# Four vector transpositions pinned to their place in the program, and three matmuls of sums for norms asked for two weight chunks later, in a four-stage decoder trunk in float32

## The chip, the cores and the metric

One core of a Trainium2 chip runs the whole program. The metric is the device time in microseconds (us) of one execution; lower is better. Three runs of the kernel before took 2047.09, 2047.10 and 2047.97 us, so the median is 2047.1 us. The profile comes from one more execution of the same program, which took 2048.53 us.

## The reference, cut to what matters

256 positions of width 2048 pass through two layers. Each layer adds to the residual `x` a mixer and a gated feed-forward network (FFN) with a causal convolution of width 3; layer 1 is the second one. A norm needs, for each position, the sum of the squares of `x` over its 2048 columns.

```python
for l in range(DEPTH):                       # DEPTH = 2
    h = rmsnorm(x, g_mix[l])
    # l = 0: chunked spatial gating, l = 1: latent attention; both beside memory attention
    x = x + concatenate([main, mo]) @ w_out[l]
    x = x + conv_ffn(rmsnorm(x, g_ffn[l]), w_ffn_up[l], conv_w[l], conv_b[l], w_ffn_down[l])
return rmsnorm(x, g_final)

def conv_ffn(h, w_up, cw, cb, w_down):       # w_up 2048 x 11264, w_down 5632 x 2048
    a = h @ w_up
    c = sum(pad(a)[:, k:k + S] * cw[k] for k in range(3)) + cb
    gate, val = c[..., :5632], c[..., 5632:]
    return (silu(gate) * val) @ w_down
```

## The kernel before, in words

**Chunks of weights.** Every large product reads its float32 weights from HBM once, in chunks of 256 x 512 numbers (512 KB). The method `chunk` (lines 93 to 118) handles one: the sync engine (SP) issues the load into a buffer `raw` (line 101), the scalar engine (ACT) writes a rounded copy `whi` (line 110; lines 115 and 116 where a gain is multiplied in), and the vector engine (DVE) writes the rest `wlo` (line 111). There are four buffers of each of the three kinds. A `raw` buffer can be loaded again when `wlo` of the chunk in it is done; a `whi` or `wlo` buffer can be written again when TensorE (PE) has finished the chunk in it.

**Products.** `gemm_fm` (line 155) multiplies a chunk pair at a time: 32 matmuls with the two `whi` (lines 147 and 148, sixteen for the first chunk and then sixteen for the second), then 16 with the two `wlo` (line 150). A product over 2048 rows and 512 columns is eight chunks, that is four pairs. In this text its chunks are called chunk 0 to chunk 7. Its result lies in two PSUM banks and is taken away after the last pair by `evict`.

**Hooks.** `gemm_fm` takes `hooks`, a table from a chunk's number to functions. They are called after the pair that holds this chunk has been written into the program, so hook 1 stands behind the first pair, hook 3 behind the second. They are how small work (scores, sums, copies) is put between chunks.

**The FFN** (`ffn`, line 582) goes through 11 groups of 512 gate columns and 512 value columns, in parts of 4, 4 and 3 groups. A group is two products with `w_ffn_up`: first the gate columns, then the value columns. Evicting a product runs `scaled` (line 228, DVE: PSUM times the norm's factor `rbc`, into `a`), one activation for each 128 columns (line 600, ACT, `c`), two multiply-adds for each (line 603, DVE, `c`), and for the value columns the product with the gate (line 616) and its split (lines 237 and 238). After a part come its products with `w_ffn_down`.

**Sums for norms.** Behind each product with `w_out` in layer 1 and layer 0, and behind each `w_ffn_down` product of layer 0's last part, DVE adds the result to the residual (line 554), and GpSimd (POOL) squares it (line 268, `sq`) and adds it to `ssum` (line 273). `rstd_bc` (line 260) adds `ssum` over the partitions by one matmul with ones (line 262; two passes in the profile) and derives `rbc` from it (lines 252 to 257, five steps on DVE and a square root on ACT, line 253). `rbc` is first read when the first product that needs it is evicted.

**The residual in token order.** The output is needed with tokens on the partitions. While `ffn` runs for layer 1, `x` is therefore transposed: `turn(h)` (line 961) has two DVE transpositions of 32 x 32 blocks (line 965) which write half `h` into the tile `small`, of which there is one buffer; `place(h, q)` (line 967) then issues 8 small transfers of 32 KB from `small` to the tile `xt`, on SP's queue (line 972). The table `turns` (line 1034) hands them to the value products of groups 1 and 2 of layer 1's FFN: `turn` at hook 0, the four `place` at hooks 1, 3, 5 and 7. That makes 4 transpositions and 64 small transfers. `xt` is first read when the first `w_ffn_down` product of layer 1 is added to it (line 978).

**Order.** What an engine executes in which order is not the written order: a scheduler simulates the program and moves an instruction ahead of others on its engine when the data it reads are there. In this kernel the transpositions depend only on the finished residual. A region marked `manual_schedule` keeps its written order, and so does a single instruction handed to `keep_in_program_order`. Each engine then runs its list strictly in order, and an instruction that waits holds up everything behind it on its engine; SP's list holds both the loads of weights and the small transfers.

Of the kernel before, what the change touches and what calls it, by code (L numbers as in the profile page):

```python
# [17 lines left out]
D = 2048  # L18
# [9 lines left out]
KR = 512  # L28
# [43 lines left out]
class Kernel:  # L72
# [510 lines left out]
    def ffn(self, l, after=None, to_tokens=None, tokens=None):  # L583
        nc, t = self.nc, self.t
        rb = self.tmp(self.cp, [P, S], "rbc", 2)
        xhl, ssum = self.xhl, self.ssum
        first = {1: [lambda: self.rstd_bc(rb, ssum, D)]}
        up, down = t["w_ffn_up"][l], t["w_ffn_down"][l]
        with self.tc.tile_pool(name=self.uid("ff"), bufs=1) as fp:
            g0 = 0  # L590
            for part, ng in enumerate(FF_GROUPS):
                h = self.ap.tile([P, NB, 512], F32R, tag="big", name=self.uid("h"))

                def conv(b, acc):
                    a = self.tmp(fp, [P, 2, S], "a", 2)
                    self.scaled(a, acc, rb)
                    c = self.tmp(fp, [P, 2, S], "c", 3)
                    for i in range(2):
                        w = lambda j: self.cT[:, l, j, b + i : b + i + 1]
                        nc.scalar.activation(c[:, i, :], a[:, i, :], AF.Identity, scale=w(2), bias=w(3))  # L600
                        for j in (1, 0):
                            o = c[:, i, 2 - j :]
                            nc.vector.scalar_tensor_tensor(o, a[:, i, : S - 2 + j], w(j), o, ALU.mult, ALU.add)  # L603
                    return c

                for g in range(g0, g0 + ng):
                    gate = self.tmp(fp, [P, 4, S], "gate", 2)

                    def eg(b, acc):
                        c = conv(4 * g + b, acc)  # L610
                        nc.scalar.activation(gate[:, b : b + 2, :], c, AF.Silu)

                    def ev(b, acc):
                        c = conv(FB + 4 * g + b, acc)
                        hv = self.tmp(fp, [P, 2, S], "hv", 2)
                        nc.vector.tensor_tensor(hv, gate[:, b : b + 2, :], c, ALU.mult)
                        j = 4 * (g - g0) + b
                        self.split_pair(h[:, j : j + 2, :], hv)

                    ks = list(range(NB))  # L620
                    turns = to_tokens[g - 1] if to_tokens is not None and g in (1, 2) else {}
                    self.gemm_fm(self.rows(up, g * 512, 512), ks, 4, lambda k: xhl[:, k, :], eg, hooks=first if g == 0 else {})
                    self.gemm_fm(self.rows(up, FF + g * 512, 512), ks, 4, lambda k: xhl[:, k, :], ev, hooks=turns)
                last = part == len(FF_GROUPS) - 1
                if last and l == 0:
                    self.new_hl()
                dn = down[g0 * 512 : (g0 + ng) * 512]
                for j in range(4):
                    src = self.rows(dn, j * 512, 512)
                    if tokens is not None:  # L630
                        self.gemm_tm(
                            src, 4 * ng, 512, lambda k: h[:, k, :], lambda tb, acc: tokens(j, tb, acc, last), late=3 if last and j == 3 else 0
                        )
                        continue

                    def ed(b, acc):
                        self.add_residual(4 * j + b, acc)
                        if last:
                            after(4 * j + b)

                    self.gemm_fm(src, list(range(4 * ng)), 4, lambda k: h[:, k, :], ed)
                g0 += ng
# [92 lines left out]
    def layer_b(self):  # L735
        nc, t, tc = self.nc, self.t, self.tc
        xhl, ssum = self.xhl, self.ssum
        rb = self.tmp(self.cp, [P, S], "rbc", 2)
        w, wkv = t["w_in_b"][0], t["w_kv_a"]
        gm = lambda k: self.gain("g_mix", NB + k)  # L740
        gk = lambda k: self.gain("g_kv", k)
        ks = list(range(NB))
        x = lambda k: xhl[:, k, :]
        mm, tt = nc.tensor.matmul, nc.vector.tensor_tensor
        with tc.tile_pool(name="lb", bufs=1) as lb:
# [8 lines left out]
            def latent(name):  # L754
                lat = lt.tile([P, 4, S], F32, name=name)
                sums = lt.tile([P, S], F32, name=name + "s")

                def evict(b, acc):
                    self.scaled(lat[:, b : b + 2, :], acc, rb)
                    self.square_add(sums, lat[:, b : b + 2, :], b == 0, self.cp)  # L760

                def finish(dst, n, gain):
                    r = self.tmp(lt, [P, S], "lr", 2)
                    self.rstd_bc(r, sums, n)
                    for b in range(4):
                        tt(lat[:, b, :], lat[:, b, :], r, ALU.mult)
                        self.split_gain(dst[:, b, :], lat[:, b, :], self.gain(gain, b))

                return evict, finish
# [8 lines left out]
                return r  # L778

            ek, fk = latent("ck")  # L780
            self.gemm_fm(self.rows(wkv, 0, KR), ks, 4, x, ek, gain=gk, hooks={1: [lambda: self.rstd_bc(rb, ssum, D)]})
            eq, fq = latent("ql")
            self.gemm_fm(self.rows(w, 0, QR), ks, 4, x, eq, gain=gm, hooks={4: [lambda: fk(chl, KR, "g_kv_lat")]})

# [21 lines left out]
            hooks = {2: [rotary_key], 5: [lambda: fq(qhl, QR, "g_q_lat")]}  # L806
# [128 lines left out]
            hooks = {0: each(attend, 8, 9) + each(turn, 10, 11), 2: each(attend, 10, 11)}  # L935
# [3 lines left out]
    def run(self):  # L939
        nc, tc, t = self.nc, self.tc, self.t  # L940
# [8 lines left out]
        with tc.tile_pool(name="fin", bufs=1) as fin:  # L949
# [9 lines left out]
            small = {}  # L959

            def turn(h):
                small[h] = self.tmp(fin, [P, 8, 2, 4, 32], "small", 1)
                for j in (0, 4):
                    src = self.x[:, 8 * h + j : 8 * h + j + 4, :].rearrange("p j s -> p (j s)")
                    nc.vector.transpose(small[h][:, j : j + 4].rearrange("p j a b c -> p (j a b c)"), src)

            def place(h, q):
                lanes = lambda i: slice(32 * i, 32 * i + 32)
# [37 lines left out]
            def tokens(j, part, acc, last):  # L1006
# [26 lines left out]
            call = lambda f, *a: lambda: f(*a)  # L1033
            turns = [
                {0: [call(turn, 0)], 1: [call(place, 0, 0)], 3: [call(place, 0, 1)], 5: [call(place, 0, 2)], 7: [call(place, 0, 3)]},
                {0: [call(turn, 1)], 1: [call(place, 1, 0)], 3: [call(place, 1, 1)], 5: [call(place, 1, 2)], 7: [call(place, 1, 3)]},
            ]
            self.ffn(1, to_tokens=turns, tokens=tokens)
# [46 lines left out]
```

## Time and profile before

| What | Value |
|---|---|
| Median of three runs | 2047.1 us (2047.09 to 2047.97) |
| The profiled execution's own time | 2048.53 us |
| Span in the profile, first to last instruction | 2046.8 us |
| PE busy | 2036.8 us |
| DVE busy | 1356.2 us |
| ACT busy | 1044.0 us |
| POOL busy | 94.2 us |
| Mean rate of the transfers | 193 GB/s |
| Mean granted TensorE clock | 0.999 |

A row of the timeline reads: start in us from the span's beginning, length in us, engine, line of the kernel, operation, what it writes and reads, count of merged instructions, and in brackets the idle time before it and what ended that. "SPq" is SP's sequencer, which issues transfers; the length there is the time of issuing, and the landing comes later. A row of the waits reads: engine and line, what it waited for, total us, number of times, longest. A row on one source line reads: line, engine, operation, names, count, then the shortest, the median and the longest duration in ns.

### The profile page before, as it was taken

The numbers are of one execution on the slowest core, as the hardware profiler recorded it, in microseconds if no ns is written. First come the engines' busy times: TensorE is split into PE (matmuls) and PEld (weight loads), VectorE is DVE, ScalarE is ACT, GpSimd is POOL, SyncE is SP. The second block draws the span as 40 slices with busy tenths as digits, with TensorE's granted clock in tenths as the row PEclk, the third lists the DMA queues.
The fourth block names the chain that finished last, engine by engine and source line by source line (L and its number), as shares of the span: only waits on it lengthen the run. The fifth ranks groups of instructions, "written<-read, shape, count | busy, mean of one in ns | idle before, by whom it ended". The sixth has DMA issues, their size and how long they took to land.

```text
span 2046.8 us, 39055 instructions
## 1 busy us (share of the span) xinstructions
PE 2036.8 (100%) x16232; PEld 1970.7 (96%) x16232; DVE 1356.2 (66%) x1859; ACT 1044.0 (51%) x1345; POOL 94.2 (5%) x125
## 2 busy tenths in 40 slices
PE   9999999999999999999999999999999999999998
PEld 8989999999999999999999999999988999889997
DVE  6855667767556666457688875776655667656665
ACT  6754644555435554345555665455544455434553
POOL 0000013000000000000052001300000000000000
PEclk9999999999999999999999999999999999999999
DMA  8675565666656666566665545786666666666654
GB/s 309 192 225 176 155 197 187 197 196 188 204 187 194 196 194 197 188 196 195 187 196 181 174 129 176 198 224 196 195 195 193 190 198 193 194 195 188 196 185 155
DMA packets 220626, 394.62 MB, mean 193 GB/s; under 512 B 31648, under 2 KB 38176, under 8 KB 220320
## 3 DMA queue, kind: packets, MB, share of 16 engines
q1 hardware_dynamic: 220160, 391.60, 62.0%
q8 instruction: 127, 2.08, 0.4%
q10 hardware_dynamic: 288, 0.52, 0.1%
q14 instruction: 51, 0.42, 0.1%
HBM read 387.88 MB, written 2.10 MB: 191 GB/s over the span
## 4 chain that ended last, share of the span: by engine, by line
PE 99%; POOL 0%; DVE 0%; issue 0%; ACT 0%; POOLq 0%
PE ps L150 26%; PE ps L147 26%; PE ps L148 26%; PE ps L178 6%; PE ps L179 6%; PE ps L180 6%; PE ps L865 0%; PE ps L485 0%; PE ps L484 0%; PE ps L487 0%; PE ps L548 0%; PE ps L513 0%; PE ps L688 0%; PE ps L898 0%; PE ps L867 0%; PE ps L288 0%
## 5 line engine op out<-in xcount | busy, mean ns | idle before, releaser
L111 DVE TENSOR_TENSOR wlo<-raw,whi 128x1024 fp32r<-128x1024 f32 (+1 forms) x672 | 817.5, 1233 | 615.7 <-issue 419.0
L110 ACT ACTIVATE whi<-raw 128x1024 fp32r<-128x1024 f32 (+1 forms) x672 | 705.2, 1056 | 800.3 <-PE ps L148 571.7
L147 PE MATMUL ps<-xhl,whi 128*128 128x256 f32 x3264 | 752.1, 277 | 0.0
L148 PE MATMUL ps<-xhl,whi 128*128 128x256 f32 x3264 | 750.6, 276 | 0.0
L147 PEld LDWEIGHTS ps<-xhl,whi 128*128 128x128 f32 x3264 | 612.8, 188 | 0.3
L148 PEld LDWEIGHTS ps<-xhl,whi 128*128 128x128 f32 x3264 | 612.6, 188 | 0.3
L150 PE MATMUL ps<-xhl,wlo 128*128 128x256 f32 x3264 | 404.3, 276 | 0.0
L150 PEld LDWEIGHTS ps<-xhl,wlo 128*128 128x128 f32 x3264 | 385.6, 188 | 0.2
L147 PE MATMUL ps<-h,whi 128*128 128x256 f32 x704 | 161.6, 276 | 0.0
L148 PE MATMUL ps<-h,whi 128*128 128x256 f32 x704 | 161.5, 276 | 0.0
L603 DVE SCALAR_TENSOR_TENSOR c<-a,cT,c 128x255 f32<-128x255 f32 (+1 forms) x352 | 146.3, 479 | 0.0
L179 PE MATMUL ps<-wlo,h 128*128 128x512 f32 (+1 forms) x364 | 139.0, 382 | 0.0
L180 PE MATMUL ps<-whi,h 128*128 128x512 f32 (+1 forms) x364 | 138.7, 382 | 0.0
L178 PE MATMUL ps<-whi,h 128*128 128x512 f32 (+1 forms) x364 | 138.3, 382 | 0.0
L147 PEld LDWEIGHTS ps<-h,whi 128*128 128x128 f32 x704 | 132.0, 188 | 0.0
L148 PEld LDWEIGHTS ps<-h,whi 128*128 128x128 f32 x704 | 131.9, 188 | 0.0
L600 ACT ACTIVATE c<-a,cT 128x256 f32<-128x256 f32 x176 | 91.6, 591 | 73.9 <-DVE a L228 73.9
L147 PE MATMUL ps<-mainhl,whi 128*128 128x256 f32 x512 | 118.0, 277 | 0.0
L148 PE MATMUL ps<-mainhl,whi 128*128 128x256 f32 x512 | 117.9, 276 | 0.0
L147 PEld LDWEIGHTS ps<-mainhl,whi 128*128 128x128 f32 x512 | 96.1, 188 | 0.0
L148 PEld LDWEIGHTS ps<-mainhl,whi 128*128 128x128 f32 x512 | 96.1, 188 | 0.0
L150 PE MATMUL ps<-h,wlo 128*128 128x256 f32 x704 | 86.9, 276 | 0.0
(246 smaller groups left out, 1973.6 us busy)
## 6 DMA issues: line engine op xcount, KB each, us to landing
raw<-in_w_ffn_up SPq DMA_DIRECT2D x352, 512.0 KB, 4.2
raw<-in_w_ffn_down SPq DMA_DIRECT2D x176, 512.0 KB, 4.7
raw<-in_w_out SPq DMA_DIRECT2D x64, 512.0 KB, 4.8
raw<-in_w_in_a SPq DMA_DIRECT2D x56, 512.0 KB, 4.3
raw<-in_w_mem_kv SPq DMA_DIRECT2D x30, 512.0 KB, 5.2
raw<-in_w_in_b SPq DMA_DIRECT2D x16, 512.0 KB, 3.9
raw<-in_w_uq SPq DMA_DIRECT2D x12, 384.0 KB, 3.2
raw<-in_w_kv_a SPq DMA_DIRECT2D x8, 512.0 KB, 3.8
```

The lines of the kernel that those rows point to most:

```text
L110: nc.scalar.activation(hi[:, :n], raw[:, :n], AF.Copy)
L111: nc.vector.tensor_tensor(lo[:, :n], raw[:, :n], hi[:, :n].bitcast(F32), ALU.subtract)
L147: mm(acc, wh, x[:, :S], start=first, stop=False)
L148: mm(acc, wh, x[:, S:], start=False, stop=False)
L150: mm(acc, wl, x[:, :S], start=False, stop=last)
L178: mm(acc, xh, wh, start=first, stop=False)
L179: mm(acc, xh, wl, start=False, stop=False)
L180: mm(acc, xl, wh, start=False, stop=last)
L600: nc.scalar.activation(c[:, i, :], a[:, i, :], AF.Identity, scale=w(2), bias=w(3))
L603: nc.vector.scalar_tensor_tensor(o, a[:, i, : S - 2 + j], w(j), o, ALU.mult, ALU.add)
```

## The change

Two hooks move from 1 to 3: the sum for the norm ahead of each FFN (used in both layers) and the one ahead of the shared key and value side. The four transpositions are handed to `keep_in_program_order`.

```diff
-        first = {1: [lambda: self.rstd_bc(rb, ssum, D)]}
+        first = {3: [lambda: self.rstd_bc(rb, ssum, D)]}
...
-            self.gemm_fm(self.rows(wkv, 0, KR), ks, 4, x, ek, gain=gk, hooks={1: [lambda: self.rstd_bc(rb, ssum, D)]})
+            self.gemm_fm(self.rows(wkv, 0, KR), ks, 4, x, ek, gain=gk, hooks={3: [lambda: self.rstd_bc(rb, ssum, D)]})
...
-                    nc.vector.transpose(small[h][:, j : j + 4].rearrange("p j a b c -> p (j a b c)"), src)
+                    tc.keep_in_program_order(nc.vector.transpose(small[h][:, j : j + 4].rearrange("p j a b c -> p (j a b c)"), src))
```

The engines' lists show what this moves. In the old list the first half was transposed and placed during the last products with `w_out` of layer 1, and the second half around the border to the FFN: on SP the 64 small transfers stood in runs of one to six between the loads. Now they stand in the two value products. SP's list in the value product of group 1, with both lists in one (minus: before; plus: after; raw_16553 and raw_16559 are the loads of its chunks 4 and 5, raw_16621 and raw_16627 those of chunks 6 and 7, raw_16718 and raw_16724 those of chunks 0 and 1 of group 2's gate product):

```order
 L101 DMA raw_16553<-in_w_ffn_up 128x2x512
 L101 DMA raw_16559<-in_w_ffn_up 128x2x512
+L972 DMA xt<-small_16474 32x8x32 x24
 L101 DMA raw_16621<-in_w_ffn_up 128x2x512
 L101 DMA raw_16627<-in_w_ffn_up 128x2x512
+L972 DMA xt<-small_16474 32x8x32 x8
 L101 DMA raw_16718<-in_w_ffn_up 128x2x512
 L101 DMA raw_16724<-in_w_ffn_up 128x2x512
```

24 small transfers now stand in one run between the loads of chunks 5 and 6, and 8 more behind chunk 7. Group 2's value product has the same, with the loads of its own chunks. On DVE, the two transpositions of a half stand between `wlo` of chunk 1 and `wlo` of chunk 2 of the same value product.

ACT's list around the border from group 1's value product to group 2's gate product (whi_16628 is chunk 7 of the value product, whi_16719, whi_16725, whi_16779 and whi_16785 are chunks 0 to 3 of the gate product, whi_16839 its chunk 4; line 600 evicts the value product):

```order
 L110 ACTIVATE whi_16628<-raw_16627 128x1024
 L110 ACTIVATE whi_16719<-raw_16718 128x1024
+L600 ACTIVATE c_16691<-a_16689,cT 128x256 x2
+L600 ACTIVATE c_16704<-a_16702,cT 128x256 x2
 L110 ACTIVATE whi_16725<-raw_16724 128x1024
 L110 ACTIVATE whi_16779<-raw_16778 128x1024
 L110 ACTIVATE whi_16785<-raw_16784 128x1024
-L600 ACTIVATE c_16691<-a_16689,cT 128x256 x2
-L600 ACTIVATE c_16704<-a_16702,cT 128x256 x2
 L110 ACTIVATE whi_16839<-raw_16838 128x1024
```

The four evicting activations moved ahead of the copies of chunks 1, 2 and 3. At the border from group 2 to group 3 they moved too, but only ahead of chunk 3.

PE's list in the first gate product of layer 1's FFN, before (ps_15608 and ps_15609 are the product's banks, wlo_15683 and wlo_15689 chunks 2 and 3):

```order
L150 MATMUL ps_15608<-xhl_14517,wlo_15683 128x256
L262 MATMUL ps_15670<-ssum_14518,ones 128x256
L150 MATMUL ps_15608<-xhl_14517,wlo_15683 128x256 x3
L150 MATMUL ps_15609<-xhl_14517,wlo_15683 128x256 x4
L150 MATMUL ps_15608<-xhl_14517,wlo_15689 128x256 x4
L150 MATMUL ps_15609<-xhl_14517,wlo_15689 128x256 x4
```

The same place now, where wlo_15672 and wlo_15678 are chunks 2 and 3:

```order
L150 MATMUL ps_15608<-xhl_14517,wlo_15672 128x256 x4
L150 MATMUL ps_15609<-xhl_14517,wlo_15672 128x256 x4
L150 MATMUL ps_15608<-xhl_14517,wlo_15678 128x256 x4
L150 MATMUL ps_15609<-xhl_14517,wlo_15678 128x256 x4
L262 MATMUL ps_15730<-ssum_14518,ones 128x256
L147 MATMUL ps_15608<-xhl_14517,whi_15742 128x256
```

The matmul of the sums went from behind the first of the pair's sixteen `wlo` matmuls to behind the last, the border of the second and third pair. In the two other places, layer 0's FFN and the key and value side, it moved to the same border.

## Prediction

> **What bounds the kernel now.** I read the head of the profile page first, then the chain that ended last, then what TensorE (PE) waited for.
>
> ```profile
> span 2046.8 us, 39055 instructions
> PE 2036.8 (100%) x16232; PEld 1970.7 (96%) x16232; DVE 1356.2 (66%) x1859; ACT 1044.0 (51%) x1345; POOL 94.2 (5%) x125
> ...
> PE 99%; POOL 0%; DVE 0%; issue 0%; ACT 0%; POOLq 0%
> ```
>
> ```profile
> PE ps L288 <- DVE ones L279: 1.1, 1, 1.1
> PE ps L262 <- POOL ssum L273: 1.0, 1, 1.0
> ```
>
> The chain is PE from end to end. Of its 10.0 us without work, one wait of 1.0 us in the middle of the program can be taken away; it is the one the change aims at. Whatever else the change does counts only if it makes PE wait where it doesn't wait now.
>
> **The moved matmuls of sums.** The timeline of PE around line 262 in layer 1, then in layer 0, then GpSimd's adds in layer 1.
>
> ```profile
> 1327.39 0.28 PE L150 MATMUL ps<-xhl,wlo 128*128 128x256 f32 x1
> 1328.71 0.70 PE L262 MATMUL ps<-ssum,ones 128*128 128x256 f32 x2 [1.04 <-POOL ssum L273]
> ```
>
> ```profile
> 359.32 0.28 PE L150 MATMUL ps<-xhl,wlo 128*128 128x256 f32 x1
> 359.44 0.59 PE L262 MATMUL ps<-ssum,ones 128*128 128x256 f32 x2
> ```
>
> ```profile
> 1325.18 3.48 POOL L273 TENSOR_TENSOR ssum<-ssum,sq 128x256 f32<-128x256 f32 x4
> ```
>
> Undisturbed, line 262 starts 0.12 us behind the matmul ahead of it (359.44 - 359.32); in layer 1 it took 1.32 us (1328.71 - 1327.39). The wait costs 1.2 us. The sums are complete at 1325.18 + 3.48 = 1328.66. The new place is fifteen matmuls later. These start 0.113 us apart by the page (32 + 16 of them fill a pair in 5.44 us: 1407.13 - 1401.69 below), so without the wait PE comes there at 1327.39 + 16 x 0.113 = 1329.2, after the sums. **Gain 1.2 us.** Layer 0 shows no wait to remove, and the third place is not in the list of waits: zero. The factor derived from the sums, in DVE's timeline:
>
> ```profile
> 1336.24 0.42 DVE L257 SCALAR_TENSOR_TENSOR rbc<-rbq,rbr 128x256 f32<-128x256 f32 x1
> ```
>
> It was ready at 1336.66, 8.0 us after line 262 began. In the new list one more `wlo` of 1.2 us stands ahead of it: 9.2 us. From the new place PE has two pairs left, 10.9 us, until the product ends whose eviction reads the factor. That hides it in all three places, so I take zero; if 1.7 us of cover are not enough somewhere, the eviction and not PE is late, since the next product has banks of its own. Bounds: zero and 1 us.
>
> **The transpositions on DVE.**
>
> ```profile
> L965 DVE STREAM_TRANSPOSE small<-xT x4: 1231/1232/1245, 1257.5 to 1325.4; 128x1024 f32<-128x1024 f32 x4
> ```
>
> ```profile
> 1379.28 2.36 DVE L111 TENSOR_TENSOR wlo<-raw,whi 128x1024 fp32r<-128x1024 f32 x2 [1.45 <-issue]
> 1384.72 1.23 DVE L111 TENSOR_TENSOR wlo<-raw,whi 128x1024 fp32r<-128x1024 f32 x1 [3.08 <-PE ps L150]
> ```
>
> In group 1's value product chunks 0 and 1 are done at 1381.64, and DVE then idles 3.08 us. Two transpositions take 2.46 us and fit: zero, and 1384.1 is when the small transfers may start. What leaves the products with `w_out` was off PE's path there, apart from the 1.2 us already counted.
>
> **The small transfers on SP, which decide.** First their issue, then one stretch of five and one of six with the loads beside them.
>
> ```profile
> L972 SPq DMA_DIRECT2D xt<-small x64: 585/608/1659, 1280.5 to 1355.9; - x64
> ```
>
> ```profile
> 1344.16 3.20 SPq L972 DMA_DIRECT2D xt<-small  x5
> 1347.46 0.55 SPq L101 DMA_DIRECT2D raw<-in_w_ffn_up  x1
> ```
>
> ```profile
> 1291.36 4.53 SPq L972 DMA_DIRECT2D xt<-small  x6
> 1295.99 0.55 SPq L101 DMA_DIRECT2D raw<-in_w_out  x1
> ```
>
> Five in a row hold SP 3.30 us up to the next load, 0.66 each; six, one of them slow, 4.63 us, 0.77 each. Before, a load stood behind every one to six of them. Now 24 stand ahead of chunk 6. What its load has to spare before the change, in SP's, ACT's and PE's timelines (the second fence is the landing of this one load, the last the start of PE's work on chunk 6 and on the next product):
>
> ```profile
> 1385.98 0.37 SPq L101 DMA_DIRECT2D raw<-in_w_ffn_up  x1
> ```
>
> ```profile
> DMA to landing us min/median/max: 3.6/3.6/3.6
> ```
>
> ```profile
> 1392.83 1.07 ACT L110 ACTIVATE whi<-raw 128x1024 fp32r<-128x1024 f32 x1 [1.45 <-PE ps L148]
> ```
>
> ```profile
> 1401.69 0.28 PE L147 MATMUL ps<-xhl,whi 128*128 128x256 f32 x1
> ...
> 1407.13 0.28 PE L147 MATMUL ps<-xhl,whi 128*128 128x256 f32 x1
> ```
>
> Chunk 6 was issued at 1385.98, landed 3.6 us later, its `whi` waited for a buffer, and PE began on it at 1401.69, 15.7 us after the issue. Landing and ACT's copy need 3.6 + 1.2 = 4.8 us (1.07 and my estimate of 0.1 for two hand-overs). So the load may be 10.9 us late (15.7 - 4.8).
>
> Now, in the old clock: the small transfers start at 1384.1 and 24 x 0.65 = 15.6 us later, at 1399.7, chunk 6 is issued. I take 0.65, near the stretch of five, since no load is mixed into the run. That is 13.7 us late: `whi` is ready at 1404.5, and **PE waits 2.8 us**. Chunk 7 goes out 0.6 us later and is needed 1.8 us later: no wait of its own. Then 8 more small transfers, 5.2 us: the next product's chunk 0 is issued at 1399.7 + 1.2 + 5.2 = 1406.1 and ready at 1410.9, while PE, 2.8 us late, is done with the pair at 1407.13 + 2.8 = 1409.95. **Second wait 0.95 us.**
>
> [...]
>
> At group 1's end the list of ACT adds a third. What stands ahead of chunk 1's copy there:
>
> ```profile
> 1407.63 1.28 DVE L228 TENSOR_TENSOR a<-ps,rbc 128x512 f32<-128x512 f32 x2
> ```
>
> ```profile
> 1408.35 2.08 ACT L600 ACTIVATE c<-a,cT 128x256 f32<-128x256 f32 x4 [1.76 <-DVE a L228]
> ```
>
> Line 600 started 1.2 us after the product's end (1408.35 - 1407.13) and takes 2.08 us. From 1409.95 and behind chunk 0's copy (1410.9) that gives 1413.0, and chunk 1's copy is done at 1414.1. PE needs it 16 matmuls, 1.8 us, after 1410.95: **third wait 1.3 us**. At group 2's end line 600 stands only ahead of chunk 3, needed 7.3 us after the product's end: zero. Group 2's value product otherwise repeats group 1's:
>
> ```profile
> 1422.80 2.36 DVE L111 TENSOR_TENSOR wlo<-raw,whi 128x1024 fp32r<-128x1024 f32 x2 [2.53 <-issue]
> 1428.24 1.23 DVE L111 TENSOR_TENSOR wlo<-raw,whi 128x1024 fp32r<-128x1024 f32 x1 [3.08 <-issue]
> ```
>
> ```profile
> 1445.21 0.28 PE L147 MATMUL ps<-xhl,whi 128*128 128x256 f32 x1
> ```
>
> DVE has the same gap, and chunk 6 is needed at 1445.21, 20.0 us after chunk 1's `wlo` (1425.16), as in group 1 (1401.69 - 1381.64 = 20.05).
>
> The sum: group 1 2.8 + 0.95 + 1.3 = 5.05; group 2 2.8 + 0.95 = 3.75; loss 8.8, gain 1.2, **net 7.6 us slower**. The profiled execution would span 2046.8 + 7.6 = 2054.4 and take 2048.5 + 7.6 = 2056.1; it lies 1.4 us above the median of the runs, so the median becomes 2047.1 + 7.6 = **2054.7 us**.
>
> Bounds: the landing of loads in this stretch,
>
> ```profile
> DMA to landing us min/median/max: 3.6/4.3/6.2
> ```
>
> is 4.3 us at the median. With that and 0.70 us an issue (between the two stretches), the first wait is 2.8 + 0.7 + 1.2 = 4.7 and the second 0.95 + 0.4 = 1.35: group 1 7.35, group 2 6.05, net +12.2, 2059.3. From below, 0.64 an issue gives a first wait of 2.6, and if everything behind it catches up nothing follows: 5.2 - 1.2 = +4.0, 2051.1.
>
> **The rivals.**
>
> *Not slower: the loads still come in time.* Chunk 6 needs its issue by 1385.98 + 10.9 = 1396.9, so 24 issues in 12.8 us, 0.53 us each, decide. Then only the gain is left: 2047.1 - 1.2 = 2045.9 us. For it: SP carried the same 64 transfers before and PE never waited for a load, and issues of a plain load take 0.37 us when SP is not pressed. Against it: the shortest of the 64 took 0.585 us, and they were spread among loads. Chance 0.10. [...]
>
> *The clock falls.* A cold PE is in the trace only at the start:
>
> ```profile
> 1.12 4.63 PE L288 MATMUL ps<-ones 128*128 128x128 f32 x20 [1.12 <-DVE ones L279]
> ```
>
> ```profile
> 6.10 0.42 PE L147 MATMUL ps<-memhl,whi 128*128 128x256 f32 x1
> 6.31 0.41 PE L148 MATMUL ps<-memhl,whi 128*128 128x256 f32 x1
> ...
> 7.28 0.63 PE L150 MATMUL ps<-memhl,wlo 128*128 128x256 f32 x4
> ```
>
> PE began at 1.12; at 6.10 its matmuls of 256 columns still started 0.21 us apart, from 7.28 on four took 0.63 us, the usual pace of 0.11. So about 6 us of work ran at half pace, 3 us lost. If the first wait of each group lets PE go cold like that, two times 3 us come on top: +13.6, 2060.7 us. For it: 2.8 us is over twice the longest wait now, and 4.7 in the upper bound. Against it: the wait of 1.04 us was not followed by a slow stretch. Chance 0.07. [...]
>
> **How the numbers follow.** My forecast, PE waiting for loads behind the small transfers, has 0.80 and spreads from 2051.1 to 2059.3; 0.03 is left for what I don't see. The range is 2051.0 to 2059.5: it holds the forecast and leaves the rest out. A measurement of this kernel can tell about 0.2% (4.1 us), so "same" is 2043.0 to 2051.2: that is the first rival and a sliver of the forecast, 0.11. Slower is 0.87: 0.79 of the forecast, 0.07 of the clock and a little of the rest. Faster has only 0.02, since no case gains 4 us.
>
> **What would show it.** Right: in the list of waits PE waits for ACT's `whi` (line 110) in group 1 and 2 and no more for `ssum`; SP's timeline has 24 small transfers in 15 to 17 us; four or five waits of PE lie between 1400 and 1460, the longest 2.5 to 5 us, at chunk 6. Wrong: chunk 6's load is issued before 1397, or PE has no wait there; or pairs behind a wait take about 11 us (the clock); or the waits lie elsewhere, on `wlo` or on the transpositions.

## The result and the profile after

Six runs of the changed kernel took 2063.43 us at the median (2060.46 to 2064.15); six of the kernel before, on the same chip, took 2047.53 us (2047.09 to 2048.95). The ratio is 1.0074, with a 95% interval of 1.0061 to 1.0087: 15.9 us slower. The forecast was 2054.7 us in a range of 2051.0 to 2059.5: the sign is right, the size is not.

The profiled execution of the changed kernel took 2062.12 us. Its head, and the shares of the chain that ended last:

```profile
span 2060.4 us, 39049 instructions
...
PE 2041.0 (99%) x16232; PEld 1973.9 (96%) x16232; DVE 1358.9 (66%) x1859; ACT 1043.7 (51%) x1345; POOL 94.4 (5%) x125
...
PE 96%; SPq 2%; DMA 1%; ACT 0%; issue 0%; DVE 0%; POOLq 0%; POOL 0%; ACTq 0%
```

The span grew by 13.6 us (2060.4 - 2046.8). PE has as many matmuls as before and is busy 4.2 us longer (2041.0 - 2036.8); the rest is idle. SP's queue and the transfers, which were not on the chain, now are. What PE waits for:

```profile
PE ps L147 <- ACT whi L110: 10.0, 3, 4.6
PE ps L288 <- DVE ones L279: 1.1, 1, 1.1
PE ps L147 <- ACT whi L132: 0.3, 1, 0.3
```

The wait for `ssum` is gone. Three waits for the `whi` of ACT's line 110, 10.0 us in all, are new. The short one at line 132 is no part of the change: an execution of the kernel before (e9 below) has 0.2 us there. SP's timeline in group 1's value product and, in the second fence, in group 2's:

```profile
1378.91 1.63 SPq L101 DMA_DIRECT2D raw<-in_w_ffn_up  x2
1382.45 17.01 SPq L972 DMA_DIRECT2D xt<-small  x24
1399.56 1.06 SPq L101 DMA_DIRECT2D raw<-in_w_ffn_up  x2
1400.67 5.22 SPq L972 DMA_DIRECT2D xt<-small  x8
1405.98 2.10 SPq L101 DMA_DIRECT2D raw<-in_w_ffn_up  x4
```

```profile
1435.30 16.32 SPq L972 DMA_DIRECT2D xt<-small  x24
1451.74 1.03 SPq L101 DMA_DIRECT2D raw<-in_w_ffn_up  x2
```

24 small transfers hold SP for 17.1 us (1399.56 - 1382.45) and 16.4 us (1451.74 - 1435.30). Only then do the loads of chunks 6 and 7 go out. This is chunk 6's load in group 1 from its issue to its landing, then ACT's timeline, then PE's:

```profile
DMA to landing us min/median/max: 4.1/4.1/4.1
```

```profile
1403.73 1.06 ACT L110 ACTIVATE whi<-raw 128x1024 fp32r<-128x1024 f32 x1 [12.06 <-DMA raw<-in_w_ffn_up]
...
1413.54 2.08 ACT L600 ACTIVATE c<-a,cT 128x256 f32<-128x256 f32 x4 [2.38 <-DVE a L228]
1415.53 1.99 ACT L110 ACTIVATE whi<-raw 128x1024 fp32r<-128x1024 f32 x2
```

```profile
1399.27 0.96 PE L150 MATMUL ps<-xhl,wlo 128*128 128x256 f32 x7
1404.84 0.58 PE L147 MATMUL ps<-xhl,whi 128*128 128x256 f32 x1 [4.61 <-ACT whi L110]
1405.22 0.42 PE L148 MATMUL ps<-xhl,whi 128*128 128x256 f32 x1
1405.43 0.41 PE L147 MATMUL ps<-xhl,whi 128*128 128x256 f32 x1
...
1410.34 0.39 PE L148 MATMUL ps<-xhl,whi 128*128 128x256 f32 x1
1410.56 0.29 PE L147 MATMUL ps<-xhl,whi 128*128 128x256 f32 x1
1410.69 0.28 PE L148 MATMUL ps<-xhl,whi 128*128 128x256 f32 x1
...
1413.07 0.28 PE L147 MATMUL ps<-xhl,whi 128*128 128x256 f32 x1
...
1416.63 0.39 PE L147 MATMUL ps<-xhl,whi 128*128 128x256 f32 x1 [1.58 <-ACT whi L110]
...
1457.04 0.39 PE L147 MATMUL ps<-xhl,whi 128*128 128x256 f32 x1 [3.84 <-ACT whi L110]
1457.26 0.28 PE L148 MATMUL ps<-xhl,whi 128*128 128x256 f32 x1
```

Issued at 1399.56, landed 4.1 us later, copied from 1403.73 to 1404.79, read by PE at 1404.84: each step waits for the one ahead of it. And PE starts again slowly. From 1404.84 its matmuls start 0.21 us apart (1405.22 to 1405.43), and only from 1410.56 on 0.11 to 0.13. The table by stretches shows the same; its columns after the length are busy time and count of PE, PEld, DVE, ACT and POOL, the granted clock, the share of the DMA engines and GB/s.

```profile
1395.00:1400.00 5.00, 5.00 (x47) 5.00 (x45) 0.00 (x0) 0.00 (x0) 0.00 (x0) 1.00 0.25 39
1405.00:1410.00 5.00, 5.00 (x24) 5.00 (x25) 2.27 (x2) 1.06 (x1) 0.00 (x0) 0.50 0.75 186
1420.00:1430.00 10.00, 10.00 (x90) 10.00 (x90) 8.94 (x10) 5.49 (x7) 0.00 (x0) 1.00 0.87 267
1457.00:1458.30 1.30, 1.26 (x11) 1.26 (x12) 1.23 (x1) 0.73 (x1) 0.00 (x0) 1.00 0.50 61
1458.40:1461.70 3.30, 3.30 (x18) 3.30 (x17) 1.23 (x1) 0.23 (x1) 0.00 (x0) 0.50 0.71 173
```

Ahead of the first wait, from 1395 to 1400, DMA moved 39 GB/s at a busy share of 0.25, while issues took SP 17.01 of the 17.1 us: the small transfers don't fill the engines, they fill SP's queue. Behind the wait the granted clock is 0.50, and 24 matmuls pass where 47 passed before. In group 2 PE starts again at 1457.04 at full clock; the clock falls only 1.3 us later and stays at 0.50 for 3.4 us. PE counts as busy there, so the list of waits shows nothing of it.

An undisturbed pair takes 5.44 us. In the changed kernel the pairs around the waits start at 1394.62, 1404.84, 1413.07 and 1420.40 in group 1 and behind it, and at 1447.60, 1457.04 and 1464.22 in group 2 and behind it. What a pair takes beyond 5.44 us is the loss, and the starts give the whole account, in us:

| Place | Forecast | Measured |
|---|---|---|
| Ahead of group 1 (wait for `ssum` gone; the rest is an earlier start) | -1.2 | -1.63 |
| Group 1, wait at chunk 6 | 2.8 | 4.78 |
| Group 1, half clock behind it | 0 | 2.79 |
| Group 1's successor, chunk 0 | 0.95 | 0 |
| The same, chunk 1 (line 600 ahead on ACT) | 1.3 | 1.89 |
| Group 2, wait at chunk 6 | 2.8 | 4.0 |
| Group 2, half clock behind it | 0 | 1.74 |
| Group 2's successor, chunk 0 | 0.95 | 0 |
| Sum | 7.6 | 13.57 |

That leaves 2.3 us between the 13.6 of the profile and the 15.9 of the medians: this execution lies 1.3 us below its median (2063.43 - 2062.12), and the profiled one of before 1.0 us above (2048.53 - 2047.53).

### The profile page after: what moved, and what is told of

It reads as the page before. It is cut to its first block, busy times and chain, and to the rows that moved or that the text cites. A ratio compares the mean times of both kernels' runs of the same rounds, so it can differ in the third digit from the quotient of the medians.

```text
span 2060.4 us, 39049 instructions
## 1 busy us (share of the span) xinstructions
PE 2041.0 (99%) x16232; PEld 1973.9 (96%) x16232; DVE 1358.9 (66%) x1859; ACT 1043.7 (51%) x1345; POOL 94.4 (5%) x125
## 4 chain that ended last, share of the span: by engine, by line
PE 96%; SPq 2%; DMA 1%; ACT 0%; issue 0%; DVE 0%; POOLq 0%; POOL 0%; ACTq 0%
PE ps L147 26%; PE ps L148 25%; PE ps L150 25%; PE ps L178 5%; PE ps L179 5%; PE ps L180 5%; SPq L972 2%; DMA raw<-in_w_mem_kv 0%; PE ps L865 0%; DMA raw<-in_w_ffn_up 0%; PE ps L548 0%; PE ps L513 0%; PE ps L485 0%; PE ps L484 0%; PE ps L487 0%
```

## The experiments

The theory: 24 issues in a row on SP make the load of chunk 6 late, PE waits for `whi`, and a wait past some length costs a slow stretch on top. Rivals: the burst of small transfers disturbs the loads in the DMA engines, not in SP's queue; the transpositions on DVE or the moved sums cost something themselves; the changed order of ACT's list does; the slow stretch comes of something else than the wait.

**The moved sums alone** (e1): the kernel before with the three hooks at 3, the transpositions not pinned.

```diff
-        first = {1: [lambda: self.rstd_bc(rb, ssum, D)]}
+        first = {3: [lambda: self.rstd_bc(rb, ssum, D)]}
...
-            self.gemm_fm(self.rows(wkv, 0, KR), ks, 4, x, ek, gain=gk, hooks={1: [lambda: self.rstd_bc(rb, ssum, D)]})
+            self.gemm_fm(self.rows(wkv, 0, KR), ks, 4, x, ek, gain=gk, hooks={3: [lambda: self.rstd_bc(rb, ssum, D)]})
```

> The kernel before with the three later hooks alone, nothing pinned. If the loss comes from the small transfers in one run on SP's queue: PE's wait of 1.0 us for ssum goes and nothing comes in its place, 1.2 to 1.6 us faster than before, about 2046.0 us. If the later sums cost something (a late eviction, a wait for the factor): slower than before, a part of the 16 us, 2050 us or more.

2047.29 us (2046.99 to 2047.87, 11 runs) against 2047.56 us (27 runs); ratio 0.9998, 0.9989 to 1.0007. Its span is 2045.6 us and its list of waits has one row:

```profile
PE ps L288 <- DVE ones L279: 1.1, 1, 1.1
```

The hooks do no harm. Their gain, 0.3 us between the medians, misses the 1.2 to 1.6 us expected and can't be told from nothing; on the wait that they were to remove see e9.

**The pin alone** (e2): the kernel before with the other part of the change.

```diff
-                    nc.vector.transpose(small[h][:, j : j + 4].rearrange("p j a b c -> p (j a b c)"), src)
+                    tc.keep_in_program_order(nc.vector.transpose(small[h][:, j : j + 4].rearrange("p j a b c -> p (j a b c)"), src))
```

> The kernel before with the four transpositions pinned, the hooks as they were. If the small transfers in one run on SP make the loss: as slow as the changed kernel, 2062 to 2065 us, with two waits of PE of 4 to 5 us at chunk 6 of the value products of groups 1 and 2; the wait for ssum may go here too, since DVE is free earlier. If the hooks have a part in the loss: clearly below 2060 us.

2061.93 us (2060.2 to 2062.82, 4 runs); ratio 1.0072, 1.0057 to 1.0088, against the same 27 runs.

```profile
PE ps L147 <- ACT whi L110: 9.4, 3, 4.5
```

```profile
1455.16 0.39 PE L147 MATMUL ps<-xhl,whi 128*128 128x256 f32 x1 [3.35 <-ACT whi L110]
```

The same three waits: the pin makes the loss by itself, 14.4 us here against 15.9 for the whole change, with ranges that overlap. By the starts of the pairs the waits at chunk 6 cost 4.67 and 3.5 us, the slow stretches behind them 1.5 and 1.7, the wait behind line 600 1.9. The second fence is the wait at chunk 6 in group 2: 3.35 us without work were followed by the half clock too, from 1455.5 to 1458.9. The wait for `ssum` is not in this list, though its hook is at 1 as before; on this see e9.

**No small transfers** (e3): the changed kernel with its transpositions on DVE and without the 64 transfers; `xt` holds zeros, so the output lacks the residual.

```diff
+            nc.gpsimd.memset(xt.rearrange("p a d -> p (a d)"), 0.0)
...
-                        nc.sync.dma_start(out=out, in_=small[h][lanes(q), :, tb, b, :])
+                        pass
```

> The changed kernel without the 64 small transfers (xt is filled with zeros instead, so the residual is left out of the output); the transpositions stay pinned. If SP's queue makes the loss: no wait of PE for whi, 1.2 to 1.6 us faster than before, about 2046 us. If the transpositions on DVE at their new place or the changed order of ACT make it: still 2055 to 2063 us.

2047.51 us (2047.31 to 2047.63, 10 runs); ratio 1.0, 0.9991 to 1.0009; span 2045.6, no wait for `whi` at line 110. The pinned transpositions cost nothing on DVE. Without the transfers the whole loss is gone. ACT's list is back in its old order here too; see the end of e8.

**The same transfers, spread** (e4): the changed kernel, with all 64 transfers on SP and pinned there a few at a time, some of them into the next group's gate product.

```diff
+            RUNS = [0, 4, 4, 4, 4, 4, 4, 8]
...
+            def piece(h, n):
+                q, b, tb = n // 8, n // 2 % 4, n % 2
...
+                tc.keep_in_program_order(nc.sync.dma_start(out=out, in_=small[h][lanes(q), :, tb, b, :]))
+
+            def run_of(h, i):
+                for n in range(sum(RUNS[:i]), sum(RUNS[: i + 1])):
+                    piece(h, n)
+
+            turns = [{0: [call(turn, h)], **{2 * i + 1: [call(run_of, h, i)] for i in range(4)}} for h in range(2)]
+            later = [{2 * i - 7: [call(run_of, h, i)] for i in range(4, 8)} for h in range(2)]
```

> The changed kernel with the same 64 small transfers on the same queue and at the same time of the program, but pinned in runs of 4 to 8 with two loads between the runs, over the value product and the next gate product. If the length of the run decides: the longest run takes 5.2 us of the 10.9 us that a load may be late, PE doesn't wait, about 2046 us. If the small transfers disturb the loads in the transfer engines wherever they stand: waits of PE in both groups, 2050 us or more.

2047.26 us (2046.65 to 2047.41, 11 runs); ratio 0.9998, 0.9989 to 1.0007; span 2045.2. SP's timeline in group 1's value product (line 1040 issues the small transfers here):

```profile
1382.44 5.31 SPq L1040 DMA_DIRECT2D xt<-small  x8
1387.84 1.06 SPq L101 DMA_DIRECT2D raw<-in_w_ffn_up  x2
1388.95 2.55 SPq L1040 DMA_DIRECT2D xt<-small  x4
1391.60 1.06 SPq L101 DMA_DIRECT2D raw<-in_w_ffn_up  x2
1392.71 2.76 SPq L1040 DMA_DIRECT2D xt<-small  x4
```

Four transfers and two loads take SP 3.8 us (1392.71 - 1388.95), less than a pair's 5.44, so the loads keep ahead. At the same number of transfers on the same queue the loss is gone with the long run.

**The transfers on another queue** (e8): the changed kernel with all 64 small transfers issued by GpSimd, the 32 of a half in one run.

```diff
-                        nc.sync.dma_start(out=out, in_=small[h][lanes(q), :, tb, b, :])
+                        nc.gpsimd.dma_start(out=out, in_=small[h][lanes(q), :, tb, b, :])
```

> The changed kernel with all 64 small transfers issued from GpSimd's queue, which is idle there; transpositions, hooks and data are the same, and the 32 of a half stand in one run with the loads flowing beside them. If the loss comes from SP being held by the issue: no wait of PE for whi, 2046.5 to 2048 us. If the burst of small transfers slows the loads in the transfer engines: waits of PE for whi in groups 1 and 2, 2050 us or more.

2047.70 us (2047.33 to 2048.01, 10 runs) against 2047.89 us (21 runs); ratio 0.9999, 0.999 to 1.0009; span 2045.8. From GpSimd's timeline:

```profile
1382.87 8.84 POOL L972 DMA_DIRECT2D xt<-small  x15 [56.97 <-DVE small L965]
1392.34 4.62 POOL L972 DMA_DIRECT2D xt<-small  x8 [0.63 <-DMA xt<-small]
```

The transfers go out at 0.59 us each from 1382.87 on, as in the changed kernel (1382.45), beside the loads, and PE has no wait for `whi`. The rival of the DMA engines falls: SP, held by issues, makes the loads late.

Something else goes along with the loss in e3, e4 and e8. As their traces show, line 600 stands behind the copy of chunk 3 again in their ACT lists, as in the kernel before. So these three take away the long run and the wait of 1.9 us behind line 600 together, and don't tell them apart. The waits at chunk 6 don't depend on that order: their load had not left SP until 1399.56.

**A shorter run** (e6, e7): the code of e4 with other counts; 20 and then 16 small transfers ahead of chunk 6, 8 behind chunk 7 and the rest behind the next product's chunk 1.

```diff
-            RUNS = [0, 4, 4, 4, 4, 4, 4, 8]
+            RUNS = [0, 0, 20, 8, 4, 0, 0, 0]
...
+            RUNS = [0, 0, 16, 8, 8, 0, 0, 0]
```

> The changed kernel with 20 small transfers ahead of chunk 6, 8 behind chunk 7 and 4 behind the next product's chunk 1, otherwise the same. If each transfer holds SP 0.65 us: the first waits shrink by 2.6 us to about 2.2 and 1.4 us, no slow pace behind them, a wait of about 1 us for chunk 0 and about 1 us for chunk 1 behind group 1; 2051 to 2055 us. If the loads are late for another reason: waits and time as in the changed kernel.

2054.36 us (2053.34 to 2056.61, 6 runs) against the 21 runs; ratio 1.0033, 1.002 to 1.0045. The wait list's row, PE's first two matmuls of chunk 6 in group 1, and the stretch behind them:

```profile
PE ps L147 <- ACT whi L110: 5.2, 4, 1.7
```

```profile
1402.18 0.38 PE L147 MATMUL ps<-xhl,whi 128*128 128x256 f32 x1 [1.71 <-ACT whi L110]
1402.40 0.28 PE L148 MATMUL ps<-xhl,whi 128*128 128x256 f32 x1
```

```profile
1402.00:1407.00 5.00, 4.73 (x39) 4.54 (x40) 2.45 (x2) 1.19 (x2) 0.00 (x0) 1.00 0.59 127
```

Four transfers fewer are 2.6 us at 0.65 each. The pairs of chunk 6 start 1.87 us (group 1) and 1.89 us (group 2) late instead of 4.78 and 4.0, that is 2.9 and 2.1 less. PE goes on at full pace at once, at clock 1.00: the wait of 1.71 us left no slow stretch. And the waits at the next product's chunk 0, which the changed kernel didn't show, are there: the pairs before it take 1.5 and 1.4 us too long (6.92 and 6.81 instead of 5.44). The time is inside the 2051 to 2055 us expected. The wait of about 1 us expected at chunk 1 behind group 1 did not come: only two of line 600's four activations stand ahead of that copy here.

> The changed kernel with 16 small transfers ahead of chunk 6, 8 behind chunk 7 and 8 behind the next product's chunk 1. By the same 0.65 us the first waits fall to nothing or under 1 us and the loads behind are at the border too; 2047 to 2050 us. If the loads are late for another reason: 2055 us or more.

2052.39 us (2052.03 to 2053.28, 10 runs); ratio 1.0023, 1.0014 to 1.0032. This missed the 2047 to 2050 us expected. SP's timeline:

```profile
1382.96 10.55 SPq L1040 DMA_DIRECT2D xt<-small  x16
1393.61 1.06 SPq L101 DMA_DIRECT2D raw<-in_w_ffn_up  x2
1394.72 5.64 SPq L1040 DMA_DIRECT2D xt<-small  x8
1400.45 1.06 SPq L101 DMA_DIRECT2D raw<-in_w_ffn_up  x2
1401.57 5.18 SPq L1040 DMA_DIRECT2D xt<-small  x8
```

Chunk 6 goes out at 1393.61, and in group 1 PE has no wait for it. But 8 transfers and two loads then take 6.85 us (1401.57 - 1394.72), over the 5.44 us of a pair, so the lateness grows from pair to pair and comes out at chunk 2 of the next product (0.8 us by the starts of the pairs). Group 2 waits 1.35 us at chunk 6, 1.38 at chunk 0 and 1.1 at chunk 2. The slack of 10.9 us is spent once; what follows has to fit a pair's time.

**PE kept at work** (e5): the changed kernel, with 16 matmuls of 128 x 128 ones between the pair of chunks 4 and 5 and that of 6 and 7, in both groups.

```diff
+            def warm():
+                acc = self.psum()
+                for i in range(16):
+                    tc.keep_in_program_order(nc.tensor.matmul(acc[:, :P], self.ones, self.ones, start=True, stop=True))
...
-                {0: [call(turn, 0)], 1: [call(place, 0, 0)], 3: [call(place, 0, 1)], 5: [call(place, 0, 2)], 7: [call(place, 0, 3)]},
+                {0: [call(turn, 0)], 1: [call(place, 0, 0)], 3: [call(place, 0, 1)], 5: [call(place, 0, 2), warm], 7: [call(place, 0, 3)]},
```

> The changed kernel with sixteen matmuls of ones by ones, about 3.4 us of work, put on PE between the pair of chunks 5 and 6 in both groups, where PE idles 4.8 and 4.0 us. If the slow pace behind the waits (2.8 and 1.7 us lost) comes from the idle time itself: chunk 6 starts when it did, the pace stays at 0.113 us a matmul, waits of about 0.9 us for the next product's chunk 0 come in its place, and the kernel gets 2 to 4 us faster than the changed one, 2059 to 2061.5 us. If the slow pace has another cause (the late buffers, the engines beside it): no faster than the changed kernel, 2063 us or more.

2060.92 us (2060.02 to 2061.84, 4 runs) against the 21 runs; ratio 1.0063, 1.0048 to 1.0078. PE's timeline at chunk 6 of group 1, and the stretch behind:

```profile
1400.50 3.73 PE L1036 MATMUL ps<-ones 128*128 128x128 f32 x32
1405.09 0.39 PE L147 MATMUL ps<-xhl,whi 128*128 128x256 f32 x1 [0.86 <-ACT whi L110]
1405.31 0.28 PE L148 MATMUL ps<-xhl,whi 128*128 128x256 f32 x1
```

```profile
1405.00:1410.00 5.00, 4.91 (x41) 4.91 (x42) 2.45 (x2) 1.10 (x2) 0.00 (x0) 1.00 0.76 157
```

Chunk 6 begins as late as in the changed kernel (1405.09 against 1404.84), but PE has filled the wait with work, and goes on at clock 1.00 with 41 matmuls in 5 us instead of 24. So it is the idle time (4.61 us in the changed kernel, 0.86 here) that brings the half clock. Group 1 loses 5.8 us instead of 9.5 (4.78 + 2.79 + 1.89). Of the 3.6 us less, 1.7 are the slow stretch less a new wait of 1.1 at chunk 0; most of the rest is not the matmuls' doing, for ACT's list has chunk 1's copy ahead of line 600 here, and the wait behind line 600 is gone. Group 2 loses 6.9 instead of 5.7: the slow stretch is gone there too, but its run of 24 began 0.87 us ahead of the product's first pair and not 1.42, so that chunk 6 cost 4.8 instead of 4.0, and waits at chunks 0 and 1 of 1.0 us each came out. The median lies 2.5 us below the changed kernel's 2063.43; each was taken beside its own runs of the kernel before, and against those the loss is 13.0 instead of 15.9 us.

**Before, once more** (e9): one further execution of the kernel before, unchanged.

> The kernel before once more, for its profile alone. The first profile had PE wait 1.0 us for ssum in an execution that took 1.4 us more than the median of the runs; the later hooks alone gained 0.3 us at the median and not 1.2. If the wait for ssum changes from execution to execution: an execution near 2047.2 us has a wait of under 0.3 us there, one near 2048.5 us again about 1 us. If the wait is the same in all of them: about 1 us whatever the time.

It took 2047.29 us, with a span of 2045.6. PE at line 262 in layer 1, and GpSimd's adds:

```profile
1327.44 0.28 PE L150 MATMUL ps<-xhl,wlo 128*128 128x256 f32 x1
1327.56 0.59 PE L262 MATMUL ps<-ssum,ones 128*128 128x256 f32 x2
```

```profile
1323.17 3.50 POOL L273 TENSOR_TENSOR ssum<-ssum,sq 128x256 f32<-128x256 f32 x4
```

The same program, without the wait: GpSimd's adds began 2.0 us earlier (1323.17 against 1325.18) and were done at 1326.67, ahead of the 1327.56 at which PE came. So the wait of 1.04 us belongs to some executions of this kernel and not to others. Of the 27 executions of the kernel before beside e1, ten took longer than the slowest of e1's eleven (2047.87 us). The later hooks may thus remove the wait where it occurs; that is suggested and not shown.

No version was shown to beat the kernel before: e1, e4 and e8 lie 0.2 to 0.3 us below it, each with 1 inside its interval. Those of e1, e3 and e4 were expected near 2046 and miss it by the gain that did not come.

## Why the prediction was wrong in size and right in sign

- **Right: the mechanism of the first waits.** Loads behind the run on SP are late and PE waits for `whi`; shown by e2 (the pin alone does it), e3 and e4 (no run, no loss), e8 (the run on another queue, no loss) and e6 (a run of 20, less loss). "Not slower: the loads still come in time" would have needed 0.53 us an issue; the median was 0.609, and a run of 24 came to 0.71 and 0.68 each.
- **Mis-sized: the first wait, 2.8 us forecast, 4.78 and 4.0 measured.** The step "I take 0.65, near the stretch of five, since no load is mixed into the run" was 1.5 us short in group 1: the row of the 64 issues had a longest one of 1659 ns, the stretch of six contained a slow one, and a run of 24 has more room for one than a run of five. One issue of the changed kernel took 1.84 us in group 1 and one 1.28 us in group 2; the others held 0.66. Landing took 4.1 instead of 3.6 us, another 0.5: the 3.6 was that of one load, while the median of the stretch, 4.3, was nearer. So 2.8 + 1.5 + 0.5 = 4.8. The upper bound, 4.7, was the better forecast.
- **The step that failed: the half clock put at nothing in the sum.** The wait and the clock were treated as separate cases, with 0.07 for the clock. That a wait of 2.8 us leaves the clock alone was the author's estimate: the longest wait in the trace of the kernel before is 1.1 us, and no profiled execution has one of 2.8. The two cases are one: the same terms that make the wait longer carry it to where the clock falls, and the forecast's own upper bound of 4.7 us lies above the 3.35 us at which e2 shows it. The half clock cost 2.79 + 1.74 = 4.5 us in the profile. Without it the profile's sum would be 9.0 us, or some 11 with the two waits at chunk 0 that e5 has in its place: both inside the forecast's 4.0 to 12.2. e5 shows that the idle time causes it, e6 that 1.7 us of it does not bring it.
  The traces set the border between two waits: 4.61, 4.51, 3.84 and 3.35 us without work (changed kernel and e2) were followed by the half clock, 1.71 us (e6) was not; between 1.71 and 3.35 nothing was run. Behind its two gaps the changed kernel's PE ran at half clock for 5.7 us (1404.84 to 1410.56) in group 1 and 3.4 in group 2.
- **The rival that came true in kind: "The clock falls", given 0.07.** Its +13.6 equals the profile's 13.57 by luck: it had 2.8 us for each first wait and 3 us for each slow stretch, where 4.78 and 4.0, 2.79 and 1.74 were measured, and 0.95 twice where nothing came.
- **Wrong, though its reason was sound: the wait at the next product's chunk 0.** Forecast 0.95 us twice, measured 0. The wait exists, as e5 and e6 show with 1.0 to 1.5 us; in the changed kernel the half clock made PE late enough for the load to come in time.
- **Right in kind: the wait behind line 600**, 1.9 instead of 1.3 us. The rows fit the step: line 600 runs from 1413.54, the copy of chunk 1 from 1415.53 to about 1416.6, PE starts at 1416.63. The load of chunk 1 had landed 4.7 us after its issue at 1406.6, that is at 1411.3; ACT idled 2.38 us for line 600 all the same, since the copy stands behind it in the list. The size came of other parts: line 600 began 0.5 us behind the product's end (1413.54 - 1413.07) and not 1.2, and no wait at chunk 0 stood ahead of it. By the forecast's own 1.2 us line 600 could not begin before 1411.15, so its 1410.9 was 0.25 us early. The order was not tried by itself; e5 and e7, where the copy of chunk 1 stands ahead of line 600, have no wait there behind group 1.
- **Wrong: the gain of 1.2 us.** It was read from one execution. e9 has no such wait, and e1 no gain beyond 0.3 us. The profiled execution lay 1.4 us above the median of the runs, which could have said so; the 1.2 us were then taken off a median that may not have held them.
- **Right: zero for the transpositions on DVE** (e3) **and for the later factor** (e1).

With waits of 4.7 and the two slow stretches of 3 us that the clock rival priced, the forecast's own rows came to 12.2 + 6 = 18, less what the slow stretches hide; the measured 13.6 (profile) and 15.9 (medians) lie between 12.2 and 18.

Open: why single issues take 0.95 to 1.9 us; where between 1.7 and 3.35 us the clock begins to fall; what the order of ACT's list costs by itself. More buffers for `raw` were not tried.

## What to carry to other kernels

Before small transfers go into a queue that also loads weights, work out two numbers: the slack of the next load (when it is needed, less its landing, the copy and its issue), against the whole run at the mean of a long run with its slow issues; and the issue time per pair against the pair's own time, which decides whether the lateness is ever made up. A wait of the engine that bounds the kernel is not priced by its length alone: where the bound of a wait's size reaches a length behind which a trace shows the clock falling (3.35 us here; behind 1.71 it did not), the slow stretch belongs in the sum. And a wait that is to be removed should be there in more than one execution before its length counts as a gain.

## What the runs showed of the hardware

- After 4.61 us without work PE ran at a granted clock of 0.50 for 5.7 us, though it was busy throughout. After 3.84 us it started at 1.00, and the clock fell to 0.50 only 1.3 us later, for 3.4 us (1458.40 to 1461.70 in the rows above).
- The cost does not follow from the wait alone: 4.61 us in the changed kernel cost 2.79 us behind it, and 4.51 us in e2 cost 1.5. In the clock records of the changed kernel the half clock at its two waits lasted 6.83 and 3.41 us and the full clock between them 47.79, which are 2, 1 and 14 times 3.41; in those of e2 it was 3.4, 3.4 and 47.8 us.
- A small transfer of 32 partitions x 8 x 128 B took SP 0.609 us to issue at the median and 0.66 from one to the next; the two loads behind a run took 1.06, 0.53 each. The DMA engines moved 39 GB/s meanwhile (1395 to 1400).
- Single issues took 0.95 to 1.9 us. The nine traces in which SP issues the small transfers have 24 issues of over 0.9 us among them, and beside 22 of these the trace has a 16 KB transfer of instructions that starts within 0.5 us of the slow issue's start, at 1394.26 us in the changed kernel, for one. A trace has 127 such transfers in some 2050 us. That is a coincidence seen 22 times, not a cause that was tested.
